# Hybrid decoder trunk on one Trainium2 core: product 2 of the second step ahead of product 5 of the first, transposes taken later, preparation held behind the last split of x

## The chip, the cores and the metric

One core of one Trainium2 chip runs the whole kernel in one launch. The metric is the device time in microseconds (us); of several executions the median counts. Five engines take part, each with an instruction queue of its own that it works off in order: TensorE (PE) multiplies, VectorE (DVE) and ScalarE (ACT) do the element work, GpSimd (POOL) and SyncE (SP) issue transfers from the chip's memory. They wait for each other through semaphores.

## The reference

Input x has 512 tokens of 1024 features in float32. Two layers follow each other; each is an FFN, a token mixer and a second FFN, each of them followed by a layer norm over a scaled residual. The first layer's mixer is block-sparse attention, the second's a causal pooling mixer.

```
for i in range(2):
    x = layer_norm(ALPHA * x + 0.5 * swiglu(x, ffn_w_gu[i, 0], ffn_w_down[i, 0]), ...)
    y = moba_attention(x, ...) if i == 0 else pool_mixer(x, ...)
    x = layer_norm(ALPHA * x + y, ...)
    x = layer_norm(ALPHA * x + 0.5 * swiglu(x, ffn_w_gu[i, 1], ffn_w_down[i, 1]), ...)

def swiglu(x, w_gu, w_down):
    g, u = split(x @ w_gu, 2)          # 1024 -> 2 * 2816
    return (silu(g) * u) @ w_down      # 2816 -> 1024
```

So there are six phases, numbered n = 0 to 5: FFN, attention, FFN, FFN, pooling, FFN. The change touches the three FFNs that are not the first: n = 2, 3 and 5.

## The kernel before, in words

**Precision.** Every operand is kept as two tiles, `hi` (the value rounded to the matmul's format) and `lo` (what is left, value minus `hi`). A product is three matmuls, L110 to L112: stationary hi with moving lo, hi with hi, lo with hi. To "split" or "prepare" an operand costs one copy on ACT (L105, `hi`) and one subtraction on DVE (L106, `lo`). Some weights are prepared without DVE ("lean", L336 to L338): ACT writes hi and minus hi, and a transfer issued by POOL adds the weight.

**Seven products instead of eight.** The up-projection is done in steps, jj = 1, 2, 3, 0, 4, 5. A step takes a 2 x 2 arrangement of blocks of x and one of the weights, and gets by with seven block products, numbered i = 1 to 7, at the price of sums of blocks. One product is two weight tiles of 128x1024; each tile is met by 12 matmuls of 128x512. Products 1 and 2 use blocks of x as they are (operands x1 and x2); 5, 6, 7 and 4 use sums of blocks that `forms` makes one after the other on DVE (L429, called from L439 to L445), each then split; product 3 uses a plain block, x3. Products 1, 6, 7 and 4 add up in one pair of PSUM banks (`BANKS` 0), 2 and later 5 with 3 in another. After 1, 6 and 5 ACT copies the banks out (`keep`, L738); after 2, 7 and 3 DVE adds a kept copy to the banks (L748), and after 2, 7, 3 and 4 `gate` (L728) makes silu(g) * u, ACT then DVE (L729, L730). The gated block is later transposed on PE by `to_features` (L753, matmuls L763) and copied out by ACT (L764). Product 6 and product 7 stand one after the other in the same banks, so 7 may start in a bank only when ACT has kept what 6 left there; in step 1 this copy is made in two halves (L737).

**Weights that are sums.** A `Quad` holds the five loads of a 2 x 2 of weights: p11, p12, s1 (a21 + a22, the second half added by a transfer that POOL issues), s3 and p22. Products 1, 2, 5, 7 and 4 use p11, p12, s1, s3 and p22; product 6 uses p11 + s1, product 3 uses p12 + (p11 + s1), both sums made in place by DVE. In steps 1 and 2 these sums are separate instructions (`apart`, L158), two for product 6 and two for product 3, since a step has two quads side by side.

**The order.** PE's queue is written out by hand: `order` (L180) lists pairs (i, jj), and the loop at L1081 issues them. ACT's, DVE's, POOL's and SP's instructions are recorded in program order and then placed by a scheduler. `run_ahead` (L345) prepares weight tiles ahead of their use and `load_ahead` loads raw tiles into 20 slots. `tc.issue_after` holds back what is recorded under it.

**The head of an FFN.** The phase before ends with layer norms for four row tiles t = 0 to 3. PE transposes each normalized tile (L487, eight 128x128 at a time), ACT and DVE scale it into the stage (`to_feature_major`, L495 and L493) and split it. Tiles 0 and 1 give x1 and x2; 2 and 3 give x3 and the blocks from which the sums are made. The transposes of tiles 2 and 3 are kept in a list `late` and taken up inside the first products by `head` (L994): one after the first weight tile of (1, 1), one after the second. Behind them PE goes through

```
before: (1,1) (2,1) (1,2) (5,1) (6,1) (7,1) (3,1) (4,1) (2,2) (6,2) ...
```

Product (1, 2) needs x1 only. Its weights are loaded as `plain` tiles, besides the quad that later loads p11 again.

Of the kernel before, what the change touches and what calls it, by code (L numbers as in the profile page):

```python
# [56 lines left out]
PARTS = 5  # L57
# [26 lines left out]
def trunk(ctx, tc, x_in, xt, rel_bias, ln_g, ln_b, w_gu, w_gq, w_dq, w_dh, w_v, a_in, a_out, b_in, b_group, b_scale, b_out, onehot, out):  # L84
# [34 lines left out]
            self.size = math.prod(src.shape[1:]) / 1024  # L119
            pieces.append(self)  # L120

    pieces, units, loaded, behind = [], [], [], {}

    def plain(src, lean=False):
        p = Piece(src)
# [52 lines left out]


    def order(eight):  # L180
        o = [(1, 1), (2, 1)] + ([(6, 1), (5, 1)] if eight else [(1, 2), (5, 1), (6, 1)])
        o += [(7, 1), (3, 1)] + [(1, 2)] * eight + [(4, 1)]
        steps = STEPS[not eight]
        for jj, following in zip(steps[1:], steps[2:] + (None,)):
            seven = [(i, jj) for i in (2, 6, 5, 7, 3, 4)]
            after = [(1, following)] if following is not None else []
            if jj == MIDDLE:
                group = [(i, FF) for i in LATER]
                o += seven[:-1] + group[:1] + seven[-1:] + group[1:] + after
            else:  # L190
                o += seven[:-1] + after + seven[-1:]
        return o + [(i, FF + 1) for i in DEEP]
# [24 lines left out]
            units.append((lambda: p.tile, (p,)))  # L217

    BY_TRANSFER = ((1, 1), (2, 1), (1, 2))

    def in_turn(quads, kinds):
        pieces[-5 * len(quads):] = [q.pieces[k] for k in kinds for q in quads]
# [18 lines left out]
    def ffn_units(l, m):  # L241
        eight = (l, m) == (0, 0)
        if eight:
            for i in FIRST:
                plain(w_gu[l, m, i])
        made = {}
        for i, jj in ORDERS[not eight]:
            lean = not eight and (i, jj) in BY_TRANSFER
            if (i, jj) == (1, 2) and not eight:
                for q in range(2):  # L250
                    plain(w_gq[l, m, 2 + q, 0], lean)
                b1 = pieces[-12:]
                pieces[-12:] = b1[0:2] + b1[4:6] + b1[2:4] + b1[10:] + b1[6:10]
                continue
            if jj not in made:
                if jj == 0:
                    made[jj] = [Quad(w_gu[l, m])]
                    pieces[-5:] = [made[jj][0].pieces[k] for k in (0, 2, 1, 3, 4)]
                elif jj == FF:
                    made[jj] = in_turn([Quad(w_dq[l, m, 0]), Quad(w_dq[l, m, 1]), narrow(Quad(w_dh[l, m]))], (0, 2, 1, 3, 4))  # L260
                elif jj == FF + 1:
                    made[jj] = in_turn([Deep(w_dq[l, m, q]) for q in (2, 3, 4)], range(5))
                else:
                    made[jj] = two_quads(w_gq[l, m], 2 * (jj - 1))
                for q in made[jj]:
                    if not eight and jj in (1, 2):
                        q.apart()
                    if i == 2:
                        q.p11.uses -= 1
            for q in made[jj]:  # L270
                q.unit(i, lean)

# [71 lines left out]

    def run_ahead(most=99):  # L345
        load_ahead()
        while len(parts) < min(len(units), taken[0] + most, retired[0] + PARTS + max(0, free() - 2) // 2 + early[0] + sum(i >= retired[0] for i in guests)):
            load_needed()
            prepare()
            load_ahead()  # L350
# [350 lines left out]
    def ffn(n, x, dest):  # L701
        with tc.tile_pool(name=f"ffn{n}", bufs=1) as fp:
# [47 lines left out]
                waiting.append((out, 4 * jj - 4 + 2 * half, h))  # L750
                return ins

            def to_features(i, kept_back=1):  # L753

                row = 0
                while i in (5, 4) and len(waiting) > (i == 4) * kept_back:
                    out, f, h = waiting.pop(0)
                    row += 1
                    turn[0] += row < 3
# [209 lines left out]
            def products(i, jj, b, amid=lambda q: None, outer=3, count=2):  # L969

                if i in (1, 2, 5):
                    accs[jj, BANKS[i]] = bank_pair(((SECOND if i != 1 else sums_at[jj]) + 4 * eight) % 8)
                acc = accs[jj, BANKS[i]]

                def one(w, k0, ts, first, last):
# [18 lines left out]
            def head(i, jj):  # L994

                def amid(q):
                    if i == 1:
                        late.pop(0)()
                    if (i, q) == (1, 1):
                        while len(parts) < taken[0] + 2:  # L1000
                            load_needed()
                            prepare()
                        with tc.issue_after(x.last.ins):
                            next(sums)
                return amid
# [32 lines left out]
            def down_second(i):  # L1038
# [34 lines left out]
                            norms.update((t, LayerNorm(n, t, 0.5, 4 if t == 3 else 2)) for t in (2, 3))  # L1073
                        early[0] = (2, 0, 4, 2, 0, 0)[n]
                if i == 1:
                    to_features(5)
                for _ in range({1: 2, 5: 1, 6: 1, 3: 2}.get(i, 0)):
                    next(operands[1])
                retire()
# [1 line left out]
            for i, jj in ORDERS[not eight]:  # L1081
                if jj == FF:
                    down_first(i)
                    to_features(i)
                    continue
                if jj > FF:
                    if last and i in (2, 4):
# [19 lines left out]
                    room(jj)  # L1107
                if jj == 0:
                    in_seven(i)
                    to_features(i)  # L1110
                    retire()
                    continue
                if not eight and (i, jj) in ((1, 1), (2, 1)):
# [5 lines left out]
                if i in DONE:  # L1119
                    ins = finish(i, jj, acc)  # L1120
                    if (i, jj) in RESIDUAL:
                        update_residual(ins)
                to_features(i, 2 if not eight and jj == 1 else 1)
                if not eight and (i, jj) in ((1, 1), (2, 1), (1, 2), (6, 1)):
                    if (i, jj) != (1, 1):
                        with tc.issue_after(x.last.ins):
                            if i == 2:
                                next(sums)
                            retire(4 if i == 2 else 2)
                            if i != 2:  # L1130
                                next(sums)
                else:
                    retire(2)
# [346 lines left out]
```

## Time and profile before

| | us |
|---|---|
| three runs | 1655.13, 1655.33, 1656.63 |
| median | 1655.33 |
| profiled execution, its own time | 1655.23 |
| its span, first to last instruction | 1653.4 |
| PE busy, share of span | 1639.1, 99% |
| DVE busy | 1362.5, 82% |
| ACT busy | 953.7, 58% |
| POOL busy | 175.3, 11% |

The profiled execution lasts 1.83 us longer than its span. PE's busy time is modelled from overlapping matmuls, so 99% does not mean that PE is at its peak; its real pace is read from the starts of its matmuls. The timeline lists each instruction with its start, its duration and, in brackets, the idle time of the engine ahead of it and what ended it. The view of waits adds these up by pairs of engines. Which tile a row of the trace handles is told by the order of the rows, since the trace leaves buffer numbers out.

### The profile page before, as it was taken

The page shows a single profiled execution, that of the slowest core. Times are in us where ns is not written, and L with a number is a line of the kernel's source. Part 1 is how long each engine was busy: PE and PEld are TensorE (multiplying, and loading weights), DVE is VectorE, ACT ScalarE, POOL GpSimd, SP SyncE. Part 2 cuts the span into 40 slices and gives each one's busy share as a digit, 9 for nine tenths or more (in the row PEclk, how much of TensorE's full clock was granted, in tenths as well). Part 3 has the DMA queues.
Part 4 walks back from the last instruction along what each step waited for, and adds up shares of the span by engine and source line. Part 5 has one row for each costly group of instructions (what it writes and reads, how often), then busy time and mean ns, then how long its engine had stood idle before and what let it go on. Part 6 is the DMA issues. An engine that isn't in the chain of part 4 may idle for free.

```text
span 1653.4 us, 21614 instructions
## 1 busy us (share of the span) xinstructions
PE 1639.1 (99%) x8057; PEld 1383.8 (84%) x8057; DVE 1362.5 (82%) x1724; ACT 953.7 (58%) x1279; POOL 175.3 (11%) x224
## 2 busy tenths in 40 slices
PE   9999999999999999999999999999999999999997
PEld 8888888898888888988888889888898878888886
DVE  7768898988675887878898878888987698779889
ACT  5555556666445665556567655556554665555562
POOL 1101101000011011101111111011000201110110
PEclk9999999999999999999999999999999999999999
DMA  9678678825157488757978897578834878966882
GB/s 304 184 227 243 155 218 227 244 69 178 52 135 197 115 240 219 202 141 211 241 204 217 248 231 185 144 214 232 224 108 125 193 204 221 243 155 169 231 210 77
DMA packets 99913, 315.62 MB, mean 191 GB/s; under 512 B 10144, under 2 KB 23496, under 8 KB 99808
## 3 DMA queue, kind: packets, MB, share of 16 engines
q1 hardware_dynamic: 71904, 214.99, 37.4%
q0 software_dynamic: 27904, 99.26, 32.7%
q8 instruction: 63, 1.03, 0.3%
q14 instruction: 42, 0.34, 0.1%
HBM read 312.09 MB, written 4.74 MB: 192 GB/s over the span
## 4 chain that ended last, share of the span: by engine, by line
PE 91%; DVE 5%; ACT 2%; issue 1%; DMA 1%; SPq 0%; DVEq 0%; ACTq 0%
PE banks L110 29%; PE banks L112 29%; PE banks L111 29%; PE banks L763 2%; DVE lo L106 1%; ACT st L495 1%; DVE x L106 1%; DVE st L429 1%; PE banks L487 1%; ACT x L105 1%; PE banks L1229 0%; DMA raw<-in_ffn_w_gu 0%; DVE st L525 0%; DVE ax L1013 0%; ACT kept L738 0%
## 5 line engine op out<-in xcount | busy, mean ns | idle before, releaser
L105 ACT ACTIVATE hi<-raw 128x1024 fp32r<-128x1024 f32 (+1 forms) x478 | 500.6, 1057 | 329.8 <-DVE lo L106 118.4
L106 DVE TENSOR_TENSOR lo<-raw,hi 128x1024 fp32r<-128x1024 f32 (+1 forms) x478 | 576.7, 1218 | 131.4 <-ACT hi L105 90.7
L110 PE MATMUL banks<-lo,x 128*128 128x512 f32 x1144 | 449.2, 393 | 2.1 <-ACT kept L738 1.1
L112 PE MATMUL banks<-hi,x 128*128 128x512 f32 x1144 | 445.7, 390 | 0.0
L111 PE MATMUL banks<-hi,x 128*128 128x512 f32 x1144 | 445.5, 389 | 0.0
L110 PEld LDWEIGHTS banks<-lo,x 128*128 128x128 f32 x1144 | 214.8, 188 | 49.3 <-ACT kept L738 3.4
L112 PEld LDWEIGHTS banks<-hi,x 128*128 128x128 f32 x1144 | 214.7, 188 | 45.2
L111 PEld LDWEIGHTS banks<-hi,x 128*128 128x128 f32 x1144 | 214.9, 188 | 43.1
L110 PE MATMUL banks<-lo,h 128*128 128x512 f32 x436 | 171.4, 393 | 0.0
L112 PE MATMUL banks<-hi,h 128*128 128x512 f32 x436 | 169.9, 390 | 0.0
L111 PE MATMUL banks<-hi,h 128*128 128x512 f32 x436 | 169.8, 389 | 0.0
L110 PE MATMUL banks<-x,hi 128*128 128x256 f32 (+1 forms) x488 | 152.8, 313 | 0.0
L112 PE MATMUL banks<-x,lo 128*128 128x256 f32 (+1 forms) x488 | 151.9, 311 | 0.8 <-DVE lo L106 0.8
L111 PE MATMUL banks<-x,hi 128*128 128x256 f32 (+1 forms) x488 | 151.7, 311 | 0.0
L304 POOL DMA_DIRECT2D raw<-in_ffn_w_gq x80 | 71.5, 901 | 650.3 <-DMA raw<-in_ffn_w_gq 175.4
L152 DVE TENSOR_TENSOR raw<-raw,raw 128x1024 f32<-128x1024 f32 (+1 forms) x86 | 102.8, 1195 | 21.0 <-DMA raw<-in_ffn_w_gq 11.8
L112 PEld LDWEIGHTS banks<-x,lo 128*128 128x128 f32 x488 | 93.0, 191 | 6.3 <-DVE lo L106 1.3
L110 PEld LDWEIGHTS banks<-x,hi 128*128 128x128 f32 x488 | 93.1, 191 | 5.6 <-DVE oT L106 0.2
L111 PEld LDWEIGHTS banks<-x,hi 128*128 128x128 f32 x488 | 93.1, 191 | 5.3
L112 PEld LDWEIGHTS banks<-hi,h 128*128 128x128 f32 x436 | 81.8, 188 | 17.3
L111 PEld LDWEIGHTS banks<-hi,h 128*128 128x128 f32 x436 | 81.9, 188 | 16.5
L110 PEld LDWEIGHTS banks<-lo,h 128*128 128x128 f32 x436 | 81.9, 188 | 16.5
(229 smaller groups left out, 2250.3 us busy)
## 6 DMA issues: line engine op xcount, KB each, us to landing
raw<-in_ffn_w_gq SPq DMA_DIRECT2D x206, 512.0 KB, 4.9
raw<-in_ffn_w_dq SPq DMA_DIRECT2D x100, 512.0 KB, 4.9
raw<-in_ffn_w_gq POOLq DMA_DIRECT2D x80, 512.0 KB, 7.1
raw<-in_ffn_w_dq POOLq DMA_DIRECT2D x52, 512.0 KB, 7.7
ax<-in_ln_b POOLq DMA_DIRECT2D x20, 512.0 KB, 8.4
raw<-in_ffn_w_gu SPq DMA_DIRECT2D x18, 512.0 KB, 5.7
raw<-in_a_w_in SPq DMA_DIRECT2D x16, 512.0 KB, 4.3
raw<-in_ffn_w_dh SPq DMA_DIRECT2D x20, 256.0 KB, 2.9
```

The source lines that it names most:

```text
L105: nc.scalar.activation(hi, src, AF.Copy)
L106: return nc.vector.tensor_tensor(lo, src, hi.bitcast(F32), op=ALU.subtract)
L110: nc.tensor.matmul(acc, sh, ml, start=first, stop=False, skip_group_check=shared)
L111: nc.tensor.matmul(acc, sh, mh, start=False, stop=False, skip_group_check=shared)
L112: nc.tensor.matmul(acc, sl, mh, start=False, stop=last, skip_group_check=shared)
L152: nc.vector.tensor_tensor(d, d, more, op=ALU.add)
L304: queued["acc"] = nc.gpsimd.dma_start(p.tile, p.plus, accum_op=ALU.add)
L429: nc.vector.scalar_tensor_tensor(out, a, scale, b, op0=ALU.mult, op1=op)
L487: nc.tensor.transpose(tp[:, i * P:(i + 1) * P], xn[:, (4 * half + i) * P:(4 * half + i + 1) * P], ident)
L495: nc.scalar.activation(src[:, i, :], tp[:, c], AF.Identity, scale=g, bias=b)
L763: nc.tensor.transpose(tp[:, c, t * P:(t + 1) * P], out[:, t, c * P:(c + 1) * P], ident)
```

## The change

Four things change in the FFNs n = 2, 3 and 5.

1. Product (2, 2) moves in `order` from behind (4, 1) to behind (1, 2). Its weights become `plain` tiles like those of (1, 2), so that each of the three FFNs loads p12 of step 2 twice: two more loads of 512 KB in each. Its result goes to the banks 6 and 7 (`TURNED`).

```
after:  (1,1) (2,1) (1,2) (2,2) (5,1) (6,1) (7,1) (3,1) (4,1) (6,2) ...
```

2. The transposes of tiles 2 and 3 are taken later (`head`): after both weight tiles of (1, 1), and after the first weight tile of (2, 1).
3. `to_features` gets the number of gated blocks that it leaves. In step 1, one block is transposed after (5, 1), one after (6, 1) and one after (4, 1); before, one after (5, 1), one after (4, 1).
4. A new list `caps` keeps `run_ahead` from preparing weights of (5, 1) and later ones until the last split of x3 is recorded.

```diff
-        o = [(1, 1), (2, 1)] + ([(6, 1), (5, 1)] if eight else [(1, 2), (5, 1), (6, 1)])
+        o = [(1, 1), (2, 1)] + ([(6, 1), (5, 1)] if eight else [(1, 2), (2, 2), (5, 1), (6, 1)])
...
-            seven = [(i, jj) for i in (2, 6, 5, 7, 3, 4)]
+            seven = [(i, jj) for i in (2, 6, 5, 7, 3, 4)][not eight and jj == 2:]
...
     BY_TRANSFER = ((1, 1), (2, 1), (1, 2))
+    HEAD = ((1, 2), (2, 2))
...
         for i, jj in ORDERS[not eight]:
+            if (i, jj) == (5, 1) and not eight:
+                caps.append(len(units))
             lean = not eight and (i, jj) in BY_TRANSFER
-            if (i, jj) == (1, 2) and not eight:
+            if (i, jj) in HEAD and not eight:
                 for q in range(2):
-                    plain(w_gq[l, m, 2 + q, 0], lean)
-                b1 = pieces[-12:]
-                pieces[-12:] = b1[0:2] + b1[4:6] + b1[2:4] + b1[10:] + b1[6:10]
+                    plain(w_gq[l, m, 2 + q, i - 1], lean)
+                if i == 2:
+                    b1 = pieces[-14:]
+                    pieces[-14:] = b1[0:2] + b1[4:6] + b1[2:4] + b1[10:] + b1[6:10]
...
-        while len(parts) < min(len(units), taken[0] + most, ...):
+        while len(parts) < min(len(units), (caps + [len(units)])[0], taken[0] + most, ...):
...
-            def to_features(i, kept_back=1):
+            def to_features(kept_back):
...
-                while i in (5, 4) and len(waiting) > (i == 4) * kept_back:
+                while len(waiting) > kept_back:
...
                 def amid(q):
-                    if i == 1:
+                    if (i, q) in ((1, 1), (2, 0)):
                         late.pop(0)()
-                    if (i, q) == (1, 1):
                         while len(parts) < taken[0] + 2:
                             load_needed()
                             prepare()
+                    if (i, q) == (2, 0):
+                        caps.pop(0)
                         with tc.issue_after(x.last.ins):
                             next(sums)
...
-                to_features(i, 2 if not eight and jj == 1 else 1)
+                opening = not eight and jj == 1
+                if i in (5, 4) or (opening and i == 6):
+                    to_features((2 if opening else 1) if i == 4 else int(opening and i == 5))
```

**What moves on PE.** In these rows x2_1 and x2_2 are the operands x1 and x2 of n = 2, w155 the second weight tile of (1, 1), w156 and w157 those of (2, 1), and the rows with ident and ax are the transposes of tiles 2 and 3. Before:

```order
L112 MATMUL banks8_74<-hi154_4575,x2_1_4695 128x512
L487 MATMUL banks8_74<-ident_76,ax_75 128x128 x8
L110 MATMUL banks8_74<-w155_4580,x2_1_4695 128x512
...
L112 MATMUL banks8_74<-w155_4580,x2_1_4695 128x512
L487 MATMUL banks8_74<-ident_76,ax_75 128x128 x8
L110 MATMUL banks8_74<-w156_4584,x2_2_4706 128x512
```

And now:

```order
L112 MATMUL banks8_74<-w155_4579,x2_1_4694 128x512
L494 MATMUL banks8_74<-ident_76,ax_75 128x128 x8
L110 MATMUL banks8_74<-w156_4583,x2_2_4705 128x512
...
L112 MATMUL banks8_74<-w156_4583,x2_2_4705 128x512
L494 MATMUL banks8_74<-ident_76,ax_75 128x128 x8
L110 MATMUL banks8_74<-w157_4587,x2_2_4705 128x512
```

Both groups of transposes stand one weight tile, 12 matmuls, later.

**What moves on DVE.** These rows begin with the sum for x6 (L429, L436 in the changed file) and the weights are named by their place: lo160 and lo161 belong to (5, 1) before, and to (2, 2) now; raw118 to raw121 are p11 and p12 of step 1, L158 the sums for products 6 and 3. Before, from the sum for x6 to the second weight tile of product 6, lo163:

```order
L429 SCALAR_TENSOR_TENSOR st2_4690<-st2_4690 128x1024
L106 TENSOR_TENSOR lo160_4911<-raw122_4532,hi160_4910 128x1024
L730 SCALAR_TENSOR_TENSOR gated2_1_2_4887<-kept2_1_1_4861,gated2_1_2_4887 128x512
L158 TENSOR_TENSOR raw118_4297<-raw118_4297,raw122_4532 128x1024
L106 TENSOR_TENSOR x2_6_4892<-st2_4690,x2_6_4892 128x1024
L106 TENSOR_TENSOR lo161_4915<-raw123_4535,hi161_4914 128x1024
L106 TENSOR_TENSOR lo162_4920<-raw118_4297,hi162_4919 128x1024
L158 TENSOR_TENSOR raw119_4303<-raw119_4303,raw123_4535 128x1024
L429 SCALAR_TENSOR_TENSOR st2_4690<-st2_4690 128x1024
L158 TENSOR_TENSOR raw120_4309<-raw120_4309,raw118_4297 128x1024
L106 TENSOR_TENSOR lo163_4953<-raw119_4303,hi163_4952 128x1024
```

Now, from the sum for x5 on; the second weight tile of product 6 is lo165:

```order
L436 SCALAR_TENSOR_TENSOR st2_4689<-st2_4689 128x1024
L755 TENSOR_TENSOR kept2_1_1_4838<-kept2_1_1_4838,banks8_74 128x1024
L106 TENSOR_TENSOR x2_5_4876<-st2_4689,x2_5_4876 128x1024
L106 TENSOR_TENSOR lo160_4910<-raw126_4566,hi160_4909 128x1024
L737 SCALAR_TENSOR_TENSOR gated2_1_2_4891<-kept2_1_1_4838,gated2_1_2_4891 128x512
L436 SCALAR_TENSOR_TENSOR st2_4689<-st2_4689 128x1024
L106 TENSOR_TENSOR lo161_4917<-raw127_4899,hi161_4916 128x1024
L106 TENSOR_TENSOR lo162_4923<-raw122_4532,hi162_4922 128x1024
L106 TENSOR_TENSOR x2_6_4896<-st2_4689,x2_6_4896 128x1024
```

```order
L106 TENSOR_TENSOR lo163_4953<-raw123_4535,hi163_4952 128x1024
L158 TENSOR_TENSOR raw118_4297<-raw118_4297,raw122_4532 128x1024
L436 SCALAR_TENSOR_TENSOR st2_4689<-st2_4689 128x1024
L755 TENSOR_TENSOR kept2_2_1_4950<-kept2_2_1_4950,banks8_74 128x1024
L106 TENSOR_TENSOR lo164_4958<-raw118_4297,hi164_4957 128x1024
L106 TENSOR_TENSOR x2_7_4964<-st2_4689,x2_7_4964 128x1024
L737 SCALAR_TENSOR_TENSOR gated2_2_2_4991<-kept2_2_1_4950,gated2_2_2_4991 128x512
L158 TENSOR_TENSOR raw119_4303<-raw119_4303,raw123_4535 128x1024
L158 TENSOR_TENSOR raw120_4309<-raw120_4309,raw118_4297 128x1024
L158 TENSOR_TENSOR raw121_4530<-raw121_4530,raw119_4303 128x1024
L106 TENSOR_TENSOR lo165_4997<-raw119_4303,hi165_4996 128x1024
```

The weights of (2, 2), its addition and its gate, the split of x7 and one more sum of weights (raw121, for product 3) now stand ahead of product 6's second weight tile. The queues of n = 5 read the same; in n = 3 one of the two weight tiles of (2, 2) is prepared ahead of this stretch, so it is shorter by one row.

More of the change, by code (lines that the diff above doesn't have):

```diff
@@ L120, in __init__ @@
             pieces.append(self)
-    pieces, units, loaded, behind = [], [], [], {}
+    pieces, units, loaded, behind, caps = [], [], [], {}, []
     def plain(src, lean=False):
@@ L269, in ffn_units @@
                         q.p11.uses -= 1
+                    if i == 6:
+                        q.p11.uses -= 1
+                        q.p12.uses -= 1
             for q in made[jj]:
@@ L346, in run_ahead @@
         load_ahead()
-        while len(parts) < min(len(units), taken[0] + most, retired[0] + PARTS + max(0, free() - 2) // 2 + early[0] + sum(i >= retired[0] for i in guests)):
+        while len(parts) < min(len(units), (caps + [len(units)])[0], taken[0] + most, retired[0] + PARTS + max(0, free() - 2) // 2 + early[0] + sum(i >= retired[0] for i in guests)):
             load_needed()
@@ L971, in products @@
                 if i in (1, 2, 5):
-                    accs[jj, BANKS[i]] = bank_pair(((SECOND if i != 1 else sums_at[jj]) + 4 * eight) % 8)
+                    accs[jj, BANKS[i]] = bank_pair(((TURNED if (i, jj) == (2, 2) and not eight else SECOND if i != 1 else sums_at[jj]) + 4 * eight) % 8)
                 acc = accs[jj, BANKS[i]]
@@ L1075, in down_second @@
                 if i == 1:
-                    to_features(5)
+                    to_features(0)
                 for _ in range({1: 2, 5: 1, 6: 1, 3: 2}.get(i, 0)):
@@ L1083, in ffn @@
                     down_first(i)
-                    to_features(i)
+                    if i in (5, 4):
+                        to_features(int(i == 4))
                     continue
@@ L1109, in ffn @@
                     in_seven(i)
-                    to_features(i)
+                    if i == 5:
+                        to_features(0)
                     retire()
@@ L1122, in ffn @@
                         update_residual(ins)
-                to_features(i, 2 if not eight and jj == 1 else 1)
-                if not eight and (i, jj) in ((1, 1), (2, 1), (1, 2), (6, 1)):
+                opening = not eight and jj == 1
+                if i in (5, 4) or (opening and i == 6):
+                    to_features((2 if opening else 1) if i == 4 else int(opening and i == 5))
+                if not eight and (i, jj) in ((1, 1), (2, 1), (1, 2), (2, 2), (6, 1)):
                     if (i, jj) != (1, 1):
                         with tc.issue_after(x.last.ins):
-                            if i == 2:
+                            if (i, jj) == (2, 1):
                                 next(sums)
-                            retire(4 if i == 2 else 2)
-                            if i != 2:
+                            retire(4 if (i, jj) == (2, 1) else 2)
+                            if i in (1, 6):
                                 next(sums)
```

## The prediction

> **What bounds the kernel now.** I read the clock first, then what PE waits for over the whole program, then the timelines of PE, ACT and DVE where it waits.
>
> ```profile
> PE 1639.1 (99%) x8057; PEld 1383.8 (84%) x8057; DVE 1362.5 (82%) x1724; ACT 953.7 (58%) x1279; POOL 175.3 (11%) x224
> core 0: 1653.4 us, clock 0.998
> PE banks L110 <- ACT kept L738: 1.1, 3, 0.5
> PE banks L110 <- DVE lo L106: 0.9, 2, 0.5
> ```
>
> PE is the bound: hardly a gap, a full clock, and the waits named are fractions of a microsecond. A change can gain only what PE loses by waiting, and a new wait of PE goes straight into the time. DVE is next with 82%, so where its work is bunched it can fall behind PE.
>
> In the timeline of PE, this is the head of n = 2: first matmul of (1, 1), the two groups of transposes (L487), and three places where the start to start distance breaks its rhythm.
>
> ```profile
> 554.25 0.39 PE L110 MATMUL banks<-lo,x 128*128 128x512 f32 x1
> ...
> 556.98 1.03 PE L487 MATMUL banks<-ident,ax 128*128 128x128 f32 x8
> ...
> 560.59 1.03 PE L487 MATMUL banks<-ident,ax 128*128 128x128 f32 x8
> ...
> 574.85 0.39 PE L112 MATMUL banks<-hi,x 128*128 128x512 f32 x1
> 575.69 0.50 PE L110 MATMUL banks<-lo,x 128*128 128x512 f32 x1 [0.45 <-DVE lo L106]
> 576.03 0.40 PE L111 MATMUL banks<-hi,x 128*128 128x512 f32 x1
> ...
> 584.25 0.39 PE L112 MATMUL banks<-hi,x 128*128 128x512 f32 x1
> 584.70 0.50 PE L110 MATMUL banks<-lo,x 128*128 128x512 f32 x1
> 585.04 0.40 PE L111 MATMUL banks<-hi,x 128*128 128x512 f32 x1
> 585.28 0.39 PE L112 MATMUL banks<-hi,x 128*128 128x512 f32 x1
> 586.14 0.50 PE L110 MATMUL banks<-lo,x 128*128 128x512 f32 x1 [0.47 <-ACT kept L738]
> ```
>
> The twelve matmuls of a weight tile take 556.98 - 554.25 = 2.73, so 0.227 each; I count 2.72 a tile. From one group of eight transposes to the next lie 3.61 = 2.72 + 0.89, so a group of eight costs 0.89 and one of four, by halving, 0.45. The waits: 575.69 - 574.85 = 0.84, that is 0.61 too long, and the matmul behind it starts 0.34 later, 0.11 too long (PE fills again): 0.72. At 584.70 it is 0.45 and 0.34: 0.33. At 586.14 it is 0.86, and 0.11 behind it: 0.74. **In n = 2 PE loses 1.79.** The first is product 5's second weight tile, late on DVE; the other two are product 7, which waits for the two halves of product 6 to be kept.
>
> The same places in n = 3, and two of the three in n = 5:
>
> ```profile
> 884.28 0.39 PE L110 MATMUL banks<-w,x 128*128 128x512 f32 x1
> ...
> 886.77 0.39 PE L112 MATMUL banks<-w,x 128*128 128x512 f32 x1
> 887.77 1.11 PE L487 MATMUL banks<-ident,ax 128*128 128x128 f32 x8 [0.61 <-DVE ax L547]
> ...
> 914.38 0.39 PE L112 MATMUL banks<-hi,x 128*128 128x512 f32 x1
> 914.92 0.50 PE L110 MATMUL banks<-lo,x 128*128 128x512 f32 x1 [0.15 <-ACT kept L738]
> ```
>
> ```profile
> 1337.99 0.50 PE L110 MATMUL banks<-lo,x 128*128 128x512 f32 x1 [0.45 <-DVE lo L106]
> ...
> 1348.48 0.51 PE L110 MATMUL banks<-lo,x 128*128 128x512 f32 x1 [0.47 <-ACT kept L738]
> ```
>
> n = 3 loses 1.00 - 0.23 = 0.77 before its first transposes, 0.08 in them (1.11 against 1.03), and 0.54 - 0.23 + 0.11 = 0.42 at product 7: 1.27. n = 5 repeats n = 2: 1.79. **In all 4.85 us, 0.29%, is the most that this change can win.**
>
> **The change part by part.** Who sets the pace is read from ACT's and DVE's rows of n = 2, ACT first.
>
> ```profile
> 557.62 2.90 ACT L495 ACTIVATE st<-banks,cols 128x128 f32<-128x128 f32 x8
> 561.09 1.01 ACT L738 ACTIVATE kept<-banks 128x1024 f32<-128x1024 f32 x1
> 562.00 1.49 ACT L495 ACTIVATE st<-banks,cols 128x128 f32<-128x128 f32 x4
> 563.37 0.65 ACT L105 ACTIVATE x<-st 128x512 fp32r<-128x512 f32 x1
> 565.91 1.06 ACT L105 ACTIVATE x<-st 128x1024 fp32r<-128x1024 f32 x1 [1.89 <-DVE st L429]
> ...
> 584.05 0.60 ACT L738 ACTIVATE kept<-banks 128x512 f32<-128x512 f32 x1 [0.81 <-PE banks L112]
> 584.55 1.05 ACT L105 ACTIVATE hi<-raw 128x1024 fp32r<-128x1024 f32 x1
> 585.50 0.59 ACT L738 ACTIVATE kept<-banks 128x512 f32<-128x512 f32 x1
> ```
>
> ```profile
> 561.82 1.36 DVE L493 TENSOR_SCALAR st<-banks,cols 128x128 f32<-128x128 f32 x4
> ...
> 564.65 1.22 DVE L429 SCALAR_TENSOR_TENSOR st<-st 128x1024 f32<-128x1024 f32 x1
> 567.00 1.23 DVE L106 TENSOR_TENSOR x<-st,x 128x1024 fp32r<-128x1024 f32 x1 [1.13 <-ACT x L105]
> 568.14 1.22 DVE L748 TENSOR_TENSOR kept<-kept,banks 128x1024 f32<-128x1024 f32 x1
> ...
> 571.54 0.69 DVE L730 SCALAR_TENSOR_TENSOR gated<-kept,gated 128x512 f32<-128x512 f32 x1
> 572.14 1.22 DVE L158 TENSOR_TENSOR raw<-raw,raw 128x1024 f32<-128x1024 f32 x1
> ...
> 584.64 1.21 DVE L158 TENSOR_TENSOR raw<-raw,raw 128x1024 f32<-128x1024 f32 x1
> ```
>
> Between the last two rows DVE runs eleven instructions of 128x1024 without a gap: 12.50 / 11 = 1.136, whatever they do; a gate takes 572.14 - 571.54 = 0.60. DVE is full from x5 on, also before the change, and the sum for x5 (564.65) opens that stretch.
>
> *Transposes later.* Both groups move behind 12 more matmuls. In n = 2 PE then goes: (1, 1) from 554.25 to 559.69, tile 2 to 560.58, one weight tile to 563.30, tile 3 to 564.19, one to 566.91. n = 3's wait for ax disappears: the transposes come at 884.28 + 5.44 = 889.72 instead of 887.77, where the tile was ready. The price is on ACT and DVE. The keep of product 1 now comes first on ACT, from 559.94 (a keep starts 0.25 behind its matmuls: product 6 is through at 584.48, its first half three matmuls earlier at 583.80, and the keep starts at 584.05) to 560.85 (562.00 - 561.09 = 0.91), the eight stage writes 2.90 to 563.75, the split of x3's first half 0.65 on ACT and 0.6 on DVE to 565.04, DVE's four stage writes 1.36 to 566.40, the second half the same way 1.3: the sum for x5 starts at 567.72. That is 4.42 behind the second transposes (563.30); before, it was 564.65 - 560.59 = 4.06. So **DVE's full stretch starts at 567.7, 3.1 later than before.** In n = 3 the same walk gives 893.33 + 4.4 = 897.73.
>
> *(2, 2) in front.* PE needs x5 5.44 later, which covers the 3.1 and DVE's wait for product 5: (1, 2) and (2, 2) fill PE from 566.91 to 577.79, product 5 to 583.23, four transposes to 583.68, product 6's first weight tile to 586.40. The work itself is no longer and no shorter; the product, its keep, addition and gate only change place. But all of it goes on DVE, ahead of product 6, in a stretch that is full. From the sum for x5 to the second weight tile of product 6 (lo165) stand seventeen instructions of 128x1024 and two gates, in the order's rows: before, twelve and one. 17 * 1.136 + 2 * 0.60 = 20.5, and 0.07 for x5, which waits for ACT (567.00 - 564.65 = 2.35 against two spacings, 2.27). lo165 starts at 567.72 + 20.6 = 588.3 and is there at 589.55. PE wants it at 586.40.
>
> On the way there are two near misses: the first weight tile of (2, 2), lo160, is there at 567.72 + 3 * 1.136 + 0.07 + 1.22 = 572.42 where PE wants it at 572.35: 0.12 with the signal and 0.11 refill; lo161 follows at 575.3 where PE, so delayed, is at 575.3. I take 0.3 for both, which moves PE to 586.7. **New wait at product 6: 589.55 - 586.7 + 0.11 = 2.95.** Behind lo165 DVE gains on PE again: product 7's weights lo166 and lo167 are there at 590.7 and 592.9, and PE wants them at 592.9 and 596.2.
>
> In n = 3 one weight tile of (2, 2) is prepared earlier: sixteen and two, 19.45 from 897.73, lo284 there at 918.4; PE wants it at 884.28 + 4 * 2.72 + 2 * 0.89 + 6 * 2.72 + 0.45 + 2.72 = 916.4. New wait 2.0 + 0.11 = 2.1, and nothing at (2, 2).
>
> *Three transposes instead of two in step 1.* The four that now stand between 6 and 7 are only moved, and cost what they cost elsewhere, 0.45. They hide the keep of product 6's first half: by 584.05 it starts 0.43 before product 6 is through (584.48) and takes 0.60. The second half isn't hidden: ACT's queue still has one hi copy of a weight between the halves, as at 584.55, so it ends 1.6 behind product 6, and PE, after 0.45 of transposes and three matmuls (0.68), is there at 1.13: 0.53 and 0.11 refill, 0.64. Before, both halves together cost 0.33 + 0.74.
>
> *Held preparation.* `caps` adds no wait in the program; it decides what the scheduler may put ahead of x3, and is in the order already. *Two more loads per FFN* are on SP's queue ahead of s3, and nobody is late for it that I find: their price is bounded below.
>
> ```profile
> raw<-in_ffn_w_gq SPq DMA_DIRECT2D x206, 512.0 KB, 4.9
> raw<-in_ffn_w_gq POOLq DMA_DIRECT2D x80, 512.0 KB, 7.1
> ```
>
> The load most in danger is s1 of step 2, which needs the slot that product 5's weights leave at 583.5: 4.9 and 7.1 later it is at 595.5, and DVE adds it after product 7's end, about 600. No cost; 4 us of cover.
>
> *The sum.* n = 2: 0.3 + 2.95 + 0.64 - 1.79 = +2.1. n = 5 the same, +2.1. n = 3: 2.1 + 0.64 - 1.27 = +1.5. Together +5.6 on the profiled 1655.23 (1653.4 and 1.83 around it), which stands 0.1 under the median: **1660.9**.
>
> *Bounds.* The sum for x5 could keep its old distance of 4.06 (0.36 less a head), lo160 cost nothing (0.3), the second half of the keep be hidden (0.64, n = 3 shows 0.42 for both halves): 1.3 less a head, in all 3.4: 1657.5. If DVE's instructions took 1.22, their whole duration, the stretch is 17 * 0.085 = 1.4 longer a head, in all 4.2: 1665; the eleven in a row speak for 1.136, so I take half, 1663.5.
>
> [...] PE would stand still for up to 2.95 us in n = 2 and 5, longer than any wait above (up to 0.77), and the head of n = 2 with three of them shows a full clock (busy times of PE, its weight loads, DVE, ACT and POOL, then the granted clock, 1.00):
>
> ```profile
> 554.00:592.00 38.00, 37.01 (x171) 29.84 (x170) 32.58 (x42) 26.57 (x38) 4.09 (x5) 1.00 0.69 186
> ```
>
> [...] My sum takes the clock as full.
>
> **The rivals.** *DVE is in time (not slower).* The two products in front give PE 5.44 more before x5; if the stretch before product 6's second weight tile is 2.95 shorter than I count (17.6 instead of 20.6, two or three instructions fewer, or a start at 564.8), no PE wait is left but the 0.64 behind product 6: -4.85 + 1.9 = -2.9, 1652.4; with that hidden too, 1650.5, faster. For it speaks that the old head had the same full DVE and lost only 0.72 to it; against it that seventeen and two is a count of rows, and eleven of them in a row kept their pace. The point at which it turns: lo165 done before 586.7.
>
> *It balances.* If lo165 is late by about 1.1 us in each head instead of 2.9, old and new waits cancel: 1655.3. That needs DVE's stretch to start near 566.
>
> *Late loads.* If another accumulating transfer stands ahead of s1 of step 2, it lands 7.1 later, at 602.6; DVE waits there with product 4's first weight tile behind it, which is then ready at 602.6 + 1.14 + 1.22 = 604.96 where PE, after products 7 and 3, wants it at 604.4: 0.6 and 0.1 a head, 1663.0.
>
> *The clock.* If PE comes out of the long wait at half speed for one weight tile, 12 matmuls cost 2.72 more in n = 2 and 5: 1666.3. The waits up to 0.6 left the clock at 1.00. [...]
>
> **How the numbers follow.** 0.2% is 3.3 us, about what a measurement can tell here: below 1652.0 is faster, above 1658.6 slower. My case, a wait at product 6, has 0.78; of that some 0.03 falls below 1658.6. In time has 0.11, split 0.05 faster and 0.06 within; balance 0.05; late loads 0.03; the clock 0.03. So slower 0.75 + 0.06 = 0.81, same 0.14, faster 0.05. The range 1657.5 to 1663.5 is my case with its bounds and leaves out the 0.22 of the others, of which its edges take in a little.
>
> **What would show it.** In PE's timeline of the changed kernel: at the second weight tile of product 6 in n = 2, 3 and 5 a wait for DVE's lo of 2 to 3 us; no wait before the first transposes of n = 3; one wait of some 0.5 for the keep in product 7, not two; a small wait at the first weight tile of (2, 2). On DVE no gap from the sum for x5 to lo165. It is wrong if product 6 has no such wait, if DVE has gaps in the stretch, or if the longest waits are elsewhere or for transfers.

## The result and the profile after

| us | kernel before | changed kernel |
|---|---|---|
| median of six runs each | 1655.78 | 1665.66 |
| lowest and highest | 1655.04 to 1656.63 | 1663.62 to 1667.69 |
| profiled execution, its span | 1655.23, 1653.4 | 1667.69, 1665.9 |
| mean granted clock of the profiled execution | 0.998 | 0.994 |

The changed kernel is slower by a factor of 1.0059 (95% interval 1.0048 to 1.0070). The direction was forecast; 1660.9 was too low by 4.8 us, and the measured median lies outside the range of 1657.5 to 1663.5.

The head of the page first: busy times, then, from the view of cores, span and clock, then the two rows of the view of waits that answer to those of before.

```profile
PE 1644.8 (99%) x8057; PEld 1387.7 (83%) x8057; DVE 1361.7 (82%) x1724; ACT 951.9 (57%) x1279; POOL 174.9 (10%) x224
core 0: 1665.9 us, clock 0.994
PE banks L110 <- DVE lo L106: 7.5, 3, 2.6
PE banks L110 <- ACT kept L745: 0.6, 2, 0.3
```

The waits have become three long ones for DVE's lo, 7.5 us in all. But PE's busy time has also grown, by 5.7 us over 1639.1 with the same 8057 instructions, and the clock is not what it was. Both are seen in PE's timeline at product 6's second weight tile in n = 2:

```profile
586.57 0.39 PE L112 MATMUL banks<-hi,x 128*128 128x512 f32 x1
589.52 0.80 PE L110 MATMUL banks<-lo,x 128*128 128x512 f32 x1 [2.56 <-DVE lo L106]
590.11 0.63 PE L111 MATMUL banks<-hi,x 128*128 128x512 f32 x1
590.54 0.63 PE L112 MATMUL banks<-hi,x 128*128 128x512 f32 x1
...
594.38 0.63 PE L112 MATMUL banks<-hi,x 128*128 128x512 f32 x1
594.80 1.06 PE L770 MATMUL banks<-ident,gated 128*128 128x128 f32 x4
595.51 0.59 PE L110 MATMUL banks<-lo,x 128*128 128x512 f32 x1
595.94 0.39 PE L111 MATMUL banks<-hi,x 128*128 128x512 f32 x1
596.17 0.39 PE L112 MATMUL banks<-hi,x 128*128 128x512 f32 x1
```

The wait is where it was forecast and as long (589.52, forecast 589.55). Behind it the matmuls start 0.43 apart, not 0.227, for the whole weight tile and the transposes; from 595.94 on the old rhythm is back. DVE ran as reckoned: the sum for x5 started at 567.66 (forecast 567.72), and the last instructions of the stretch are lo165's sum, the two sums for product 3 and lo165 with lo166:

```profile
567.66 1.22 DVE L436 SCALAR_TENSOR_TENSOR st<-st 128x1024 f32<-128x1024 f32 x1
...
584.83 3.50 DVE L158 TENSOR_TENSOR raw<-raw,raw 128x1024 f32<-128x1024 f32 x3
588.24 2.36 DVE L106 TENSOR_TENSOR lo<-raw,hi 128x1024 fp32r<-128x1024 f32 x2
```

The same place in n = 3 and in n = 5, and behind each the wait for the second half of product 6's keep:

```profile
920.48 0.39 PE L112 MATMUL banks<-hi,x 128*128 128x512 f32 x1
923.23 0.65 PE L110 MATMUL banks<-lo,x 128*128 128x512 f32 x1 [2.35 <-DVE lo L106]
...
926.66 0.48 PE L112 MATMUL banks<-hi,x 128*128 128x512 f32 x1
926.97 0.39 PE L110 MATMUL banks<-lo,x 128*128 128x512 f32 x1
...
929.25 0.50 PE L110 MATMUL banks<-lo,x 128*128 128x512 f32 x1 [0.29 <-ACT kept L745]
...
1360.00 0.54 PE L110 MATMUL banks<-lo,x 128*128 128x512 f32 x1 [2.56 <-DVE lo L106]
...
1363.75 0.39 PE L110 MATMUL banks<-lo,x 128*128 128x512 f32 x1
...
1366.03 0.50 PE L110 MATMUL banks<-lo,x 128*128 128x512 f32 x1 [0.29 <-ACT kept L745]
```

Cut at the moments where the clock changes, the view of stretches gives for n = 2 (columns as in the prediction; the seventh number behind the stretch's bounds, ahead of the DMA share, is the granted clock):

```profile
585.51:588.92 3.41, 1.45 (x7) 0.85 (x5) 3.41 (x4) 2.77 (x3) 0.87 (x1) 1.00 0.49 166
588.92:592.33 3.41, 2.81 (x7) 2.24 (x8) 3.41 (x4) 0.18 (x1) 0.87 (x1) 0.50 0.84 264
592.33:595.74 3.41, 3.41 (x12) 2.73 (x11) 0.94 (x2) 1.98 (x3) 0.00 (x0) 0.50 1.02 253
595.74:599.15 3.41, 3.41 (x16) 2.79 (x16) 2.50 (x3) 3.30 (x5) 0.00 (x0) 1.00 1.06 284
```

The clock is 1.00, then half for two stretches of 3.41 us, then 1.00. In n = 3 and n = 5 it is half for one such stretch:

```profile
920.01:923.42 3.41, 1.06 (x5) 0.57 (x4) 3.41 (x4) 2.74 (x3) 0.88 (x1) 1.00 0.51 184
923.42:926.83 3.41, 3.41 (x9) 2.64 (x9) 3.16 (x3) 0.00 (x0) 0.87 (x1) 0.50 0.82 193
...
1356.91:1360.32 3.41, 0.85 (x4) 0.41 (x3) 3.41 (x4) 2.68 (x3) 0.87 (x1) 1.00 0.57 185
1360.32:1363.73 3.41, 3.41 (x9) 2.65 (x8) 3.03 (x3) 0.00 (x0) 0.86 (x1) 0.50 0.82 197
```

Four stretches of 3.41 us at half clock take 4 * 3.41 * 0.5 / 1665.9 = 0.004 off the mean clock, the step from 0.998 to 0.994. What the kernel before lacks to 1.000 lies in its tail, where PE has nothing left to do: its clock is 0.50 from 1648.33 to 1651.74, behind the last matmul.

The account of the profiled execution, each term from the rows above or from PE's timeline in the same way, with 0.227 a matmul and 0.11 refill as in the prediction:

| us | n = 2 | n = 3 | n = 5 | forecast (2, 3, 5) |
|---|---|---|---|---|
| waits of before, gone | -1.79 | -1.27 | -1.79 | the same |
| first weight tiles of (2,2) | 0.34 | 0 | 0.29 | 0.3, 0, 0.3 |
| wait at product 6, with refill | 2.83 | 2.63 | 2.82 | 2.95, 2.1, 2.95 |
| matmuls at half clock | 2.90 | 1.58 | 1.59 | 0 |
| second half of the keep | 0 | 0.57 | 0.56 | 0.64 each |
| sum | 4.28 | 3.51 | 3.47 | 2.1, 1.5, 2.1 |

The half-clock term of n = 2: from 589.52 to 595.94 lie 6.42 us; at full clock that is 0.34 for the first matmul, 11 * 0.227, 0.45 for the transposes and 0.23: 3.52. For n = 3, 926.97 - 923.23 = 3.74 against 0.34 + 8 * 0.227 = 2.16. The three sums are 11.3 of the 12.5 that the span grew; of the rest some 0.4 lies in n = 4 and 0.8 behind the last matmul. The clock is 6.1 of them.

### The profile page after: what moved, and what is told of

It reads as the page before. It is cut to its first block, busy times and chain, and to the rows that moved or that the text cites. A ratio compares the mean times of both kernels' runs of the same rounds, so it can differ in the third digit from the quotient of the medians.

```text
span 1665.9 us, 21653 instructions
## 1 busy us (share of the span) xinstructions
PE 1644.8 (99%) x8057; PEld 1387.7 (83%) x8057; DVE 1361.7 (82%) x1724; ACT 951.9 (57%) x1279; POOL 174.9 (10%) x224
## 4 chain that ended last, share of the span: by engine, by line
PE 87%; DVE 9%; ACT 2%; issue 1%; DMA 0%; SPq 0%; DVEq 0%; ACTq 0%
PE banks L110 28%; PE banks L112 28%; PE banks L111 28%; DVE lo L106 2%; PE banks L770 2%; DVE x L106 1%; DVE st L436 1%; DVE st L532 1%; ACT st L502 1%; DVE ax L1021 1%; DVE raw L158 1%; PE banks L494 1%; PE banks L1241 0%; DVE kept L755 0%; DVE st L500 0%
```

## The experiments

The theory: the changed kernel's wait is the one that was forecast, and what comes on top is the clock, which PE's standing still has halved. The main rival: the matmuls behind the wait are slow for another reason in that stretch. Times are medians. Each group of runs had the kernel before beside it on the same chip: 1655.35 for the eight unread matmuls, the held additions, the transposes at their old places and the later transposes alone, 1656.24 for the two unread matmuls, product 7 bank by bank and the two versions at the end. Runs of different groups are compared by their distance from it.

### Eight unread matmuls in the wait

```diff
+            def fill(q):
+                if q == 0:
+                    o = x.parts[6]
+                    for _ in range(8):
+                        nc.tensor.matmul(bank(TURNED + (turn[0] + 1) % 2, "idle"), o[:, 0, 0, 0:P], o[:, 0, 0:2, :], start=True, stop=True)
...
+                elif not eight and (i, jj) == (6, 1):
+                    acc = products(i, jj, of_x(x.parts[i]), fill)
```

> The changed kernel, with eight matmuls of 128x512 whose result nobody reads put on PE behind product 6's first weight tile of step 1, into a bank that is free there, in n = 2, 3 and 5: 8 * 0.227 = 1.8 us of PE's wait of 2.75 to 2.95 are filled, the operand is not there any earlier. Theory (the clock): PE's idle stretch is what halves its clock, so the wait stays as long for the data, the matmuls behind it keep 0.227 us, the mean clock goes back to 0.998, and the time falls by the half-speed windows of the changed kernel, on average 2.2 a run at 1.5 us: about 1662.2. Rival (the matmuls behind the wait are slow for another reason, such as traffic in that stretch): no change, 1665.7, clock 0.996.

Measured: 1661.38 (1661.26 to 1662.18, five runs), clocks 0.998 and 0.999, 6.0 above the kernel before where the changed kernel was 9.9 above it. PE's timeline in n = 2, the eight in one row:

```profile
587.62 0.39 PE L112 MATMUL banks<-hi,x 128*128 128x512 f32 x1
587.85 1.97 PE L1019 MATMUL banks<-x 128*128 128x512 f32 x8
590.52 0.50 PE L110 MATMUL banks<-lo,x 128*128 128x512 f32 x1 [0.70 <-DVE lo L106]
590.86 0.39 PE L111 MATMUL banks<-hi,x 128*128 128x512 f32 x1
591.09 0.40 PE L112 MATMUL banks<-hi,x 128*128 128x512 f32 x1
```

From the last matmul ahead of the wait to the first behind it lie 2.90, as in the changed kernel (2.95): the data come no earlier. Yet the next matmuls are 0.23 apart. The same wait for data, with PE busy in it for 1.97 us, left the clock full. This rules the rival out and shows the cause, and since the run took back only the half-clock matmuls, it also measures the forecast's sum without them: +6.0 against +5.6.

### Two unread matmuls in the wait

The same edit with `range(2)`.

> As the run with eight unread matmuls behind product 6's first weight tile, but with two: 0.45 us of the wait filled, so PE stands idle for about 2.1 us in n = 2 and 5 and 1.9 in n = 3, between the 1.5 of the run with the held additions, where the clock stayed full, and the 2.35 to 2.56 of the changed kernel, where it fell. Theory (the clock falls when most of a fixed window of 3.41 us, which runs on regardless of the program, is idle): it depends on where the wait lies in the window, so fewer half-speed windows than the changed kernel's 2.2 a run, 0.3 to 1.3, differing from run to run: 1661.8 to 1663.4. Rival (a sharp length of wait between 2.1 and 2.35): none, 1661.4. Rival (any wait over 1.6): 2 or more, 1664.5.

Measured: 1664.55 (1662.15 to 1665.57, five runs), clocks 0.997 four times and 0.998 once. Beside its own kernel before that is +8.3. Counted in the same way from 1655.35, the expected range was about +6.5 to +8, the first rival's time +6 and the second's +9.1: the time lies just above the range and below the second rival. The trace speaks against both rivals. First PE's waits in n = 2 and n = 3 of this run, then its stretches of 3.41 us about the waits of n = 2, n = 3 and n = 5:

```profile
590.33 0.50 PE L110 MATMUL banks<-lo,x 128*128 128x512 f32 x1 [2.10 <-DVE lo L106]
...
923.17 0.50 PE L110 MATMUL banks<-lo,x 128*128 128x512 f32 x1 [1.90 <-DVE lo L106]
```

```profile
587.47:590.88 3.41, 1.31 (x6) 0.78 (x5) 3.41 (x4) 2.44 (x3) 0.87 (x1) 1.00 0.54 178
590.88:594.29 3.41, 3.41 (x9) 2.63 (x8) 2.80 (x3) 0.17 (x1) 0.88 (x1) 0.50 0.85 214
...
918.56:921.97 3.41, 2.71 (x12) 1.88 (x10) 3.41 (x5) 2.82 (x5) 0.41 (x1) 1.00 0.55 166
921.97:925.38 3.41, 2.21 (x10) 1.83 (x11) 3.41 (x5) 0.73 (x1) 1.19 (x2) 1.00 0.90 275
...
1355.47:1358.88 3.41, 1.29 (x7) 0.75 (x6) 3.41 (x4) 2.63 (x3) 0.87 (x1) 1.00 0.52 177
1358.88:1362.29 3.41, 3.41 (x10) 2.67 (x9) 2.98 (x3) 0.00 (x0) 0.87 (x1) 0.50 0.85 193
```

Behind the wait of 2.10 in n = 2 the clock was 0.50, and in n = 5 behind a stretch with 2.12 idle (3.41 - 1.29); behind the wait of 1.90 in n = 3 it stayed at 1.00. The two drops of this run are 1358.88 - 590.88 = 768.00 apart, 225 * 3.4133. In the changed kernel's run the drops have the same spacing: 923.42 - 588.92 = 334.50 = 98 * 3.4133, 1360.32 - 588.92 = 771.40 = 226 * 3.4133. Counted on from 590.88, 97 * 3.4133 leads to 921.97, the middle of the wait in n = 3: the two rows there have 0.70 and 1.20 idle. So in these two traces the outcome goes with the idle time within one stretch of that spacing (1.96 to 2.56 ahead of the five drops in the heads) and not with the length of the wait alone; what lies behind that is not shown, and that the window of the theory runs on regardless of the program is shown only as far as this common spacing goes. The expectation had 0.3 to 1.3 half-speed windows a run; the profiled run had two. How often a wait of 2.1 halves the clock is not shown. The +2.3 over the run with eight unread matmuls is one to two half-clock stretches of some 1.6; that the four runs without a trace lost them in this way is not shown.

### The additions for product 3 held back

```diff
+            def held_add(d, more):
+                with tc.issue_after(queued["split"].ins):
+                    return add(d, more)
...
-                        3: (lambda: add(self.p12, self.p11), (self.p12, self.p11))}
+                        3: (lambda: held_add(self.p12, self.p11), (self.p12, self.p11))}
...
-                split(hi[:, c], lo[:, c], src[:, c])
+                queued["split"] = split(hi[:, c], lo[:, c], src[:, c])
```

> The changed kernel, with the two additions for product 3 of step 1 held behind the last prepared lo ahead of them, so that they stand behind product 6's second weight tile on DVE: its lo then waits only for its hi on ACT and comes 1.1 us earlier, 588.4 instead of 589.5 in n = 2. Theory (the clock): waits shrink from 2.75 to 2.95 to 1.7 to 1.9, 3.2 us in all; if so short a wait leaves the clock alone another 3.3 go, about 1659; if not, 1662.4. Rival (waits alone count, the slow matmuls come with the stretch): 1662.5 with the clock at 0.996.

Measured: 1660.45 (1660.08 to 1663.13, five runs), clocks 0.998 and 0.999. The two waits of n = 2 in PE's timeline:

```profile
588.93 0.50 PE L110 MATMUL banks<-lo,x 128*128 128x512 f32 x1 [1.52 <-DVE lo L106]
...
604.34 0.50 PE L110 MATMUL banks<-lo,x 128*128 128x512 f32 x1 [1.00 <-DVE lo L106]
```

The wait at product 6 shrank by 1.0, about as expected, and with an idle 1.5 us the clock stayed full in all three heads of the profiled run; the other four runs have the mean clock of the kernel before. But 1.0 to 1.3 a head came back as a wait at product 4's first weight tile, since the additions that now stood late pushed back what was behind them on DVE. So of the 4.8 that this kernel is better than the changed one (+5.1 against the kernel before instead of +9.9) most is the clock, 3.9 by the run with eight unread matmuls. That the two sums stand in lo165's way is confirmed; they would have to go to a better place.

### The transposes back at their old places

```diff
-                    if (i, q) in ((1, 1), (2, 0)):
+                    if i == 1:
                         late.pop(0)()
+                    if (i, q) in ((1, 1), (2, 0)):
                         while len(parts) < taken[0] + 2:
```

> The changed kernel with the transposes of tiles 2 and 3 back at their old places, inside (1,1), everything else kept: product (2,2) stays in front. DVE's full stretch then starts 3.1 us earlier and the lo of product 6's second weight tile is there at about 586.5, where PE wants it: the wait there falls to some 0.1 to 0.4. Left are n = 3's wait for ax (0.85) and the second half of product 6's keep (0.6 a head). Theory: n = 2 and 5 gain 1.05 each on the kernel before, n = 3 loses 0.45: about 1654.1, clock 0.998. Rival (the slow matmuls come with the order of the products): 1657 to 1658 with the clock below 0.998.

Measured: 1657.06 (1655.93 to 1658.16, eleven runs), 1.0011 of the kernel before (1.0002 to 1.0019). The long wait with its half clock is gone, so the later transposes are what makes product 6 that late; but the time is 3 us above the expected one. The first two DVE rows of the stretch and PE's wait in n = 2 show why:

```profile
563.91 1.22 DVE L436 SCALAR_TENSOR_TENSOR st<-st 128x1024 f32<-128x1024 f32 x1
566.26 1.22 DVE L106 TENSOR_TENSOR x<-st,x 128x1024 fp32r<-128x1024 f32 x1 [1.13 <-ACT x L105]
```

```profile
585.49 0.39 PE L112 MATMUL banks<-hi,x 128*128 128x512 f32 x1
587.04 0.50 PE L110 MATMUL banks<-lo,x 128*128 128x512 f32 x1 [1.16 <-DVE lo L106]
```

In the changed kernel the addition for product 2 stands between the sum for x5 and its split and fills the time in which ACT writes x5's hi; here the split stands right behind the sum, and DVE waits 1.13 for ACT. lo165 is late by as much in n = 2 and 5; with refill that is 1.43 each where 0.1 to 0.4 was expected, 2.1 to 2.7 of the 3 us. A count of rows needs the order in which they stand.

### The later transposes alone

The kernel before with the new conditions in `head` and nothing else:

```diff
-                    if i == 1:
+                    if (i, q) in ((1, 1), (2, 0)):
                         late.pop(0)()
-                    if (i, q) == (1, 1):
                         while len(parts) < taken[0] + 2:
                             load_needed()
                             prepare()
+                    if (i, q) == (2, 0):
                         with tc.issue_after(x.last.ins):
```

> The kernel before with the transposes of tiles 2 and 3 at their new, later places alone; product (2,2) stays behind (4,1). DVE starts 3.1 us later with the old stretch. By the count of DVE's rows the lo of product 5's second weight tile is 0.3 late, that of product 6's first 1.3, and product 7's two waits for the keep stay at 1.07: 2.7 a head against 1.79, 1.79 and 1.27. Theory: about 1655.8 + 3.2 = 1659, clock 0.998, since no wait is as long as 2 us. Rival (later transposes alone cause the changed kernel's loss): a wait of 2.5 or more behind (1,2), half-speed matmuls, 1663 to 1666.

Measured: 1666.64 (1665.09 to 1670.52, five runs), clocks 0.995 to 0.998. My count missed: the wait at product 6's first weight tile is there (1.08), but two follow that I hadn't counted, 0.86 at product 3's second weight tile and 3.26 at product 4's first. DVE's row ahead of the last, and PE's three, in n = 2:

```profile
599.25 1.23 DVE L158 TENSOR_TENSOR raw<-raw,raw 128x1024 f32<-128x1024 f32 x1 [3.33 <-DMA raw<-in_ffn_w_gq]
```

```profile
580.24 0.50 PE L110 MATMUL banks<-lo,x 128*128 128x512 f32 x1 [1.08 <-DVE lo L106]
...
595.38 0.50 PE L110 MATMUL banks<-lo,x 128*128 128x512 f32 x1 [0.86 <-DVE lo L106]
...
601.67 0.50 PE L110 MATMUL banks<-lo,x 128*128 128x512 f32 x1 [3.26 <-DVE lo L106]
```

DVE stood 3.33 us at an addition for step 2 whose transfer had not landed, with the first weight tile of product 4 behind it, and PE waited 3.26 for that, with matmuls 0.43 apart after it. That is the mechanism that the prediction had as the rival "late loads", in another kernel than the one it was priced for. Why the transfer came late is not shown. One step of it may be that POOL issued a transfer at 590.46, right behind a lo on DVE that its row names, where the kernel before issued the one in that place at 585.42. The wait at product 4 is in n = 5 too (2.48), not in n = 3, and behind both the clock fell (in n = 5 to 0.50 from 1370.38 to 1373.79), here in the old order of products, so it isn't bound to the new one.

The runs so far separate two parts of the change. Beside the kernel before, (2, 2) in front with the transposes at their old places costs 1.7, the later transposes alone 11.3, both 9.9. So the later transposes are the costly part, in either order of products. The third transpose of step 1 and the held preparation (`caps`) were not run apart from (2, 2).

### Product 7 bank by bank

The run with eight unread matmuls, and in `products`:

```diff
+                    kt = [(k, t) for k in range(ks) for t in ts]
+                    if (i, jj) == (7, 1) and not eight:
+                        kt.sort(key=lambda o: o[1])
-                    for k in range(ks):
-                        for t in ts:
+                    for k, t in kt:
```

> The run with eight unread matmuls, and in product 7 of step 1 all six matmuls of a weight tile into the first bank ahead of the six into the second. Theory: the second half of product 6's keep, for which PE waits 0.57 with refill in each head, then has three matmuls (0.68) more cover and is hidden: 3 * 0.57 = 1.7 less than 1661.4, so 1659.7. Rival: the wait only goes elsewhere, no change, 1661.4.

Measured: 1659.90 (1658.79 to 1660.84, ten runs), 3.7 above the kernel before in place of 6.0: 2.4 less, where 1.7 were expected. In its trace no wait for the keep is left in any of the three heads. The term was real, and it is cheap to hide.

### A version without the waits

The transposes at their old places and product 7 bank by bank, as above, and two edits more:

```diff
+                if (i, jj) == (2, 2) and not eight:
+                    with tc.issue_after(x.last.ins):
+                        retire(2)
                 if i in (1, 6, 5):
                     keep(i, jj, acc)
...
-                        3: (lambda: add(self.p12, self.p11), (self.p12, self.p11))}
+                        3: (lambda: held_add(self.p12, self.p11), (self.p12, self.p11))}
```

Here `held_add` waits for the split of product 6's second weight tile only, not for product 7's.

> The run with the transposes at their old places and (2,2) in front, with three things more: preparation is released ahead of the addition and gate of (2,2); the additions for product 3 of step 1 stand behind product 6's second weight tile on DVE; product 7 goes bank by bank. Theory: of 2.0 lost in n = 2 and in n = 5 some 0.2 to 0.4 is left, in n = 3 the wait for ax (0.85): the kernel before loses 1.79, 1.27, 1.79, so about 3 less than it: 1652.3, clock 0.998. Rival: the additions held back make product 3's or 4's weights late, as they did in the run that held them behind product 7's: no better than 1655.4.

Measured: 1652.70 (1651.89 to 1654.13, eleven runs), 0.9981 of the kernel before (0.9972 to 0.9990). At product 6 in n = 2 PE now goes from 586.07 to 586.57, 0.27 more than its rhythm, and its only named wait in the three heads is n = 3's 0.6 for ax.

### The same with n = 3's transposes together

```diff
                     if i == 1:
-                        late.pop(0)()
+                        for _ in range(2 * q if n == 3 else 1):
+                            late.pop(0)()
```

> The run before this one in the list, with both groups of transposes of n = 3 alone one behind the other after (1,1), where ax is ready. Theory: the wait of 0.85 goes, and DVE's start there, about 1.5 us later, still leaves product 6's second weight tile in time: 0.8 less, 1651.5. Rival: the later start brings a wait of the same size back at product 6: no change, 1652.3.

Measured: 1651.94 (1651.16 to 1652.79, eight runs), 0.9974 of the kernel before (0.9964 to 0.9985): 4.3 us faster than the kernel before and 0.8 faster than the version without this edit, as expected, though the runs of the two overlap. So the new order need not cost anything. That it is what gains the 4.3 is not shown: product 7 bank by bank was not tried in the kernel before, whose waits for the keep cost 1.07, 0.42 and 1.07 by the prediction's rows, together 2.6 of its 4.85.

## Why the prediction was wrong

*The places and lengths of the waits: right.* lo165 at 589.52 (589.55 forecast), DVE's start at 567.66 (567.72), the small wait at (2, 2) 0.34 and 0.29 (0.3), no wait left at n = 3's transposes, one wait for the keep instead of two in n = 3 and 5. Without the clock the change costs 6.0 (the run with eight unread matmuls), against 5.6.

*The step that failed: "My sum takes the clock as full", and with it the 0.03 for the rival of the clock.* The drop was listed, at 2.72 a head (measured: 1.58 and 1.59 where one stretch was at half clock, 2.90 where two were), and taken for unlikely. That a wait of 2.95 leaves the clock full was the author's estimate and no run shows it: the rows of before had no wait above 0.77 in a head, and a clock of 1.00 with those. The changed kernel's waits of 2.56, 2.35 and 2.56 us were each followed by half clock, with 1.96 us idle in the stretch ahead of the drop in n = 2, and beside these a forecast wait of 2.95 makes the clock the likely case. That the rival's time, 1666.3, is so near the measured 1665.66 is partly luck: it has 2.72 in two heads, 5.4 in all, where the median lost about 3.9 and the profiled run 6.1 in three heads. In the profiled run this term is 6.1 us, in the median of the six runs about 9.9 - 6.0 = 3.9.

*n = 3's wait was 0.5 too short.* The count of sixteen and two was right, but DVE stood still once, waiting for ACT's half of x6's split, which is not a matter of counting:

```profile
909.99 1.23 DVE L106 TENSOR_TENSOR x<-st,x 128x1024 fp32r<-128x1024 f32 x1 [0.47 <-ACT x L105]
```

*The keep's second half* cost 0.57 where 0.64 was forecast, and nothing in n = 2 of the profiled run, where PE, its matmuls 0.43 apart at half clock, came to that bank at 596.40, behind the copy's end at 595.79.

*The range* was built from the bounds of the waits alone. With one stretch at half clock in each head, 3 * 1.58 = 4.7, it would have reached to 1668 and held the time. Two slips in the sums are small beside that: 2.1 + 2.1 + 1.5 is 5.7, not 5.6, and half of 4.2 above 1660.9 is 1663.0, not 1663.5.

## What to carry to other kernels

Where a change leaves TensorE waiting in one piece as long as here (waits of 2.10 to 3.26 us were followed by half clock, those of 1.52 and 1.90 were not), price the clock with the wait: here 1.6 us for one stretch of 3.41 us at half clock and 2.9 for two, and not the same number in every run. Eight matmuls that nobody reads, put into an unavoidable wait, kept the clock at 0.998 to 0.999 here and cost nothing, since they ended before the data came; with two the clock fell in n = 2 and n = 5. When work is pulled forward in the order of the engine that sets the pace, count what then stands in front of it on the engine that feeds it, and look for what there isn't urgent: with the transposes early (in n = 3 together), preparation released sooner, two additions behind the urgent tile and product 7 bank by bank, the same order of products went from +9.9, or +6.0 without the clock's share, to -4.3.

## What the runs showed of the hardware

All of this is read from the traces of these runs, and what decides on the clock inside the chip is not shown by them.

In the heads of the changed kernel and of the run with two unread matmuls the clock was at half for one stretch of 3.41 us at a time, once for two (588.92 to 595.74). Within a run the drops there were whole multiples of 3.4133 us apart: in the changed kernel those of n = 3 and n = 5 came 98 and 226 such lengths behind that of n = 2, in the run with two unread matmuls the two are 225 lengths apart.

The clock fell behind stretches in which PE was idle for 1.96, 2.35 and 2.56 us (changed kernel), 2.10 and 2.12 (two unread matmuls), and behind waits of 3.26 and 2.48 (later transposes alone). It didn't fall where a wait of 1.90 lay with 0.70 in one stretch and 1.20 in the next, nor behind a wait of 1.52 (the additions held back, n = 2). The first two rows here are from the tail of the version without the waits, behind the last matmul: 1.79 idle (3.42 - 1.63), and the clock of the next stretch is still 1.00. So, by the profile's busy time, the least idle time ahead of a drop was 1.96 us of a stretch and the most without one 1.79; no stretch that was read lies in between.

```profile
1640.16:1643.58 3.42, 1.63 (x13) 1.39 (x12) 3.42 (x10) 0.00 (x0) 0.00 (x0) 1.00 0.31 119
1643.58:1646.99 3.41, 0.00 (x0) 0.00 (x0) 3.20 (x10) 0.20 (x1) 0.00 (x0) 1.00 0.09 35
...
1370.38:1373.79 3.41, 3.00 (x7) 2.42 (x8) 3.41 (x4) 0.75 (x2) 0.00 (x0) 0.50 1.07 211
1373.79:1377.21 3.42, 3.42 (x16) 2.81 (x16) 3.42 (x5) 1.90 (x2) 0.00 (x0) 1.00 0.08 14
```

Behind a half-clock stretch that was busy for 2.81 of 3.41 us the clock stayed at 0.50 (n = 2 of the changed kernel); behind one that was busy for 3.00 (the last two rows, n = 5 of the later transposes alone) and behind those that were busy for all 3.41 (n = 3 and n = 5 of the changed kernel) it was 1.00 again. From start to start 128x512 matmuls lie 0.427 apart at half clock ((594.38 - 590.54) / 9 in n = 2 of the changed kernel) and 0.227 at full.

Counted from the program's first instruction, the drop of n = 2 came at 588.92 in the changed kernel's trace and at 590.88 in that of the run with two unread matmuls, 1.96 us apart and so not a multiple of 3.4133. By estimate from these two, the same wait can fall into one stretch in one run and be divided between two in the next. This would fit the spread of the six runs of the changed kernel, with clocks of 0.994 to 0.997 and times of 1667.69 to 1663.62 where the kernel before varied by 1.6 us; how many stretches at half clock each of them had was read in the profiled one alone.
